# Low parts of half of the up projection's weights by an accumulating DMA instead of GpSimd subtractions

## The chip, the cores and the metric

One core of one Trainium2 chip runs the whole kernel in one launch. The metric is the device time of that launch in microseconds (us). The kernel before took 1085.0 us, the median of three runs (1084.67 to 1085.46 us).

## What is computed

The reference is one layer of an encoder trunk over 512 tokens of width 1024, all in float32: token mixing (a Mamba-2 branch and a windowed attention branch, merged by gates), then channel mixing. The change touches the channel mixing alone, a squared-ReLU MLP with an inner width of 4096:

```
h = rmsnorm(x, pre_mlp_norm[l])
f = jnp.square(jax.nn.relu(h @ w_mlp_in[l])) @ w_mlp_out[l]
x = x + rmsnorm(f, post_mlp_norm[l])
```

`h @ w_mlp_in` is called the up projection (weights 1024 x 4096) and the product with `w_mlp_out` (4096 x 1024) the down projection.

## The kernel before

**Split products.** TensorE multiplies in the type `fp32r`, whose values hold fewer bits than float32. So each float32 operand is split in two: a high part `hi`, the value rounded to `fp32r`, and a low part `lo = value - hi`. A product of two split operands is three matmuls (`mm3`, L404; the matmul itself is issued at L398): high times high, high times low, low times high. For weights, ScalarE (ACT) makes the high part by a cast, and GpSimd (POOL) the low part by a subtraction.

**Up projection.** `up_quantum` (L1491) computes one block of 128 of the 4096 inner columns for all 512 tokens. Its weights are one chunk: 1024 x 128 values, held as a tile of 128 partitions x 1024 (eight blocks of 128 rows side by side), 512 KB. SyncE (SP) loads the chunk into a raw tile `wr` (`chunk_raw`, L445). `chunk_split` (L455) casts it into `wh` (L473) and subtracts into `wl` in four pieces of 128 x 256 (L477). Then `cm` (L527) runs 24 matmuls of 128 x 512 into one PSUM bank `pp`: for each of eight blocks two with `wh` and one with `wl`. So the first matmul that needs `wl` is the third of the 24. `up_done` (L1441) applies the squared ReLU and `combine` (L1457) prepares and splits the operands of the down projection.

**Down projection.** It runs in four parts of 1024 inner columns. Each part is seven products of a fast 2 x 2 block multiplication (`fold`, L1522; a product is 24 matmuls into PSUM banks `ps`), with weight chunks made of raw tiles `wd`, or of `wt`, differences of those; their casts stand at L1571 and their subtractions at L1575.

**Stages.** The up blocks 0 to 7 are computed first. Then the seven products of down part 0 alternate with the up blocks 8 to 15, those of part 1 with blocks 16 to 23, those of part 2 with blocks 24 to 31, and part 3 runs alone at the end. Blocks 16 to 23 lie at about 863 to 956 us of the profile, blocks 24 to 31 at about 956 to 1038 us.

**Buffers.** `wr`, `wh` and `wl` are rings of three buffers each (`RAW` and `SPL` are 3). A chunk can be cast only when TensorE has used the chunk that stood in the same buffer of the ring for the last time, three chunks earlier. Some down chunks are held in other buffers (`twin`) and are made long before they are used.

**Order.** After all instructions are recorded, `Planner` (L77) orders them on every engine by its own model of costs: `depend` (L156) finds what each instruction waits for and in which order the buffers of a ring are taken, `duration` (L205) gives a cost, and `plan` (L264) plays the program through. TensorE's matmuls are taken in program order among those that the model has ready. The order is then fixed, and each engine runs its own list in order.

In the tables below names of buffers carry numbers: `wl_905` is the low part of one chunk, `wh_904` its high part, `pp_911` the bank into which it is multiplied.

Of the kernel before, what the change touches and what calls it, by code (L numbers as in the profile page):

```python
# [10 lines left out]
F32 = mybir.dt.float32  # L11
F32R = mybir.dt.float32r
AF = mybir.ActivationFunctionType
ALU = mybir.AluOpType
# [12 lines left out]
SLOTS, RAW, SPL, PP, AHEAD, SPARE = 67, 3, 3, 3, 4, 6  # L27

LO_MIX = "vp"
LO_DOWN = "p", "p", "p", "vp"  # L30
WARM = 13
LO_V = "pvpvpvpv"
# [44 lines left out]
class Planner:  # L77
# [77 lines left out]

    def depend(self):  # L156
        self.pre = [set() for _ in self.ins]
        live, users, ring, seen, first, base = {}, {}, {}, {}, {}, {}
        self.turn = [set() for _ in self.ins]
        for n, i in enumerate(self.ins):  # L160
            for write, aps in ((False, i.ins), (True, i.outs)):
                for ap in self.operands(aps):
                    name = ap.tensor.name
                    if name.startswith(("in_", "out_")):
                        continue
                    if name not in users:
                        users[name], live[name] = set(), []
                        if name in self.tags:
                            tag, bufs = self.tags[name]
                            held = ring.setdefault(tag, [])  # L170
                            held.append(name)
                            if len(held) > 1:
                                self.turn[n].add(first[held[-2]])
                            first[name] = n
                            if len(held) > bufs:
                                base[name] = users[held[-1 - bufs]]
                                live.pop(held[-1 - bufs])
                    key = (name, ap.offset, tuple(map(tuple, ap.ap)))
                    if key not in seen:
                        seen[key] = self.region(ap)  # L180
                    p0, p1, m = seen[key]
                    kept = []
                    psum = name.startswith(("ps_", "pp_"))
                    for u, w, q0, q1, k in live[name]:
                        hit = q0 < p1 and p0 < q1 and k & m
                        if u != n and (hit and (w or write) or psum):
                            self.pre[n].add(u)
                        if not (u != n and (psum or write and hit and p0 <= q0 and q1 <= p1 and k & ~m == 0)):
                            kept.append((u, w, q0, q1, k))
                    if name in base and not any(u in self.pre[n] for u, *_ in live[name]):  # L190
                        self.pre[n] |= base[name]
                    kept.append((n, write, p0, p1, m))
                    live[name] = kept
                    users[name].add(n)
        self.post, self.next = [[] for _ in self.ins], [[] for _ in self.ins]
        for n, p in enumerate(self.pre):
            p.discard(n)
            self.turn[n] -= p
            self.turn[n].discard(n)
            for u in p:  # L200
                self.post[u].append(n)
            for u in self.turn[n]:
                self.next[u].append(n)

    def duration(self, n):  # L205

        i, e = self.ins[n], self.eng[n]
        outs, ins = self.operands(i.outs), self.operands(i.ins)
        size = lambda ap: math.prod(d[1] for d in list(ap.ap)[1:])
        w = max([size(a) for a in outs + ins])  # L210
        psum = any(a.tensor.name.startswith(("ps_", "pp_")) for a in outs + ins)
        kind = type(i).__name__
        if e == "PE":
            w = size(outs[0])
            if ins[0].dtype == F32R:
                return 13.5 + w / 2.4, False
            c = (2.2 + w / 1.2) if i.is_transpose else (4.4 + w / 0.6)
            return (c / 2 if i.tile_size[1] == 64 and outs[0].ap[0][1] == 64 else c), False
        if e == "SP":
            return (600 if list(outs[0].ap)[0][1] == 64 else 375), False  # L220
        wide = sum(1 for a in ins if size(a) == w and w > 1)
        columns = sum(1 for a in ins if size(a) == 1 and w > 1)
        if e == "ACT" and "DMA" in kind:
            return 400, False
        if e == "ACT":
            c = (170 if psum else 205) + 0.82 * w + (175 if len(outs) > 1 else 0)
            return c + (85 if columns else 0) * (w < 512 or columns > 1), False
        if e == "POOL":
            if "pow" in str(getattr(i, "op", "")):
                return (1020 if w > 1 else 545), True  # L230
            return (190 if w <= 4 else 180 + 2.15 * w), bool(ins)
        if wide >= 2:
            return 158 + 1.04 * w + (45 if columns else 0), not psum
        if kind == "InstTensorScalarPtr" and not psum:
            return 220 + 0.51 * w, True
        return 150 + 1.04 * w, False
# [27 lines left out]
    def plan(self, wait=0.3):  # L264
# [8 lines left out]
        free = dict.fromkeys(self.OVERLAP, 0.0)  # L273
        port = {"DVE": 0.0, "POOL": 0.0}
        queue, kind, landed = 0.0, None, []
        order, self.when = {e: [] for e in self.OVERLAP}, {}
        for _ in self.ins:
            best = None
            for e, some in avail.items():
                if some:  # L280
                    t = max(free[e], min(ready[n] for n in some))
                    if best is None or t < best[0]:
                        best = t, e
            t, e = best
            some = avail[e]
            if e == "PE":
                n = self.next_matmul(some, ready, t, kind)
            else:
                n = min((n for n in some if ready[n] <= t), key=lambda n: (key[n], n))
                m = min(some, key=lambda n: (key[n], n))  # L290
                if ready[m] <= t + wait * self.cost[n][0]:
                    n = m
            some.remove(n)
            order[e].append(n)
            t = self.when[n] = max(t, ready[n])
            c, locks = self.cost[n]
            c *= 2 if e == "PE" and t < self.COLD else 1
            end = t + c
            if e == "SP":
                queue = max(queue, t + self.LEAD) + self.transfer(n)  # L300
                free[e], end = end, queue + self.TAIL
                landed.append(end)
                if len(landed) >= 8:
                    free[e] = max(free[e], sorted(landed)[-8])
            elif e == "PE":
                end += self.change(kind, self.kind[n])
                kind = self.kind[n]
                free[e], end = end, end + 160
            else:
                if locks:  # L310
                    other = "POOL" if e == "DVE" else "DVE"
                    end += max(0.0, port[other] - t - 145)
                    port[e] = end
                free[e] = end - self.OVERLAP[e]
                end += 2500 if "DMA" in type(self.ins[n]).__name__ else 0
            for s in self.post[n]:
                same = self.eng[s] == e == "PE"
                ready[s] = max(ready[s], free[e] if same else end + self.AFTER[self.eng[s]])
                left[s] -= 1
                if not left[s]:  # L320
                    avail[self.eng[s]].append(s)
            for s in self.next[n]:
                ready[s] = max(ready[s], t)
                left[s] -= 1
                if not left[s]:
                    avail[self.eng[s]].append(s)
# [12 lines left out]
class Trunk:  # L339
# [115 lines left out]
    def chunk_split(self, i):  # L455
        if len(self.chunks[i]) == 2:
            self.parts[i] = self.chunks[i][1](i in self.ring)
            return
        _, kk, n, eng = self.chunks[i]
        raw = self.raw.pop(i)  # L460
        m = kk * n
        hi = self.wp.tile([128, 1024], F32R, tag="wh", name=self.name("wh"), bufs=SPL)
# [8 lines left out]
        lo = self.wp.tile([128, 1024], F32R, tag="wl", name=self.name("wl"), bufs=SPL)  # L471
        self.tags[lo.tensor.name] = "wl", SPL
        self.nc.scalar.copy(hi[:, :m], raw)  # L473
        engines = {"v": self.nc.vector, "p": self.nc.gpsimd}
        for e, c in zip(eng, range(0, m, m // len(eng))):
            c = slice(c, c + m // len(eng))
            engines[e].tensor_tensor(lo[:, c], raw[:, c], hi[:, c].bitcast(F32), op=ALU.subtract)  # L477
        v = lambda t: t[:, :m].rearrange("p (k n) -> p k n", k=kk)
# [1010 lines left out]
        return 8 * part + n // 2 + 4 * (n % 2)  # L1489

    def up_quantum(self, i):  # L1491
        return self.cm(self.d_w_mlp_in[0], self.block(i) * 128, lambda: self.h2, lambda ps: self.up_done(ps, i))

    def up_halves(self, n):

# [250 lines left out]
```

## Time and profile before

| | |
|---|---|
| median of three runs | 1085.0 us |
| the profiled execution itself | 1085.44 us |
| its span, first to last instruction | 1083.7 us |
| DVE (VectorE) busy | 785.1 us, 72% |
| ACT (ScalarE) busy | 654.4 us, 60% |
| POOL (GpSimd) busy | 808.1 us, 75% |
| moved by DMA | 152.21 MB, mean 140 GB/s |

The profile is of one execution. Busy time is what an engine spent on instructions. A PE (TensorE) matmul is shown with 0.39 us, from its start to its modelled end, and matmuls overlap; the time that one adds is the distance from one start to the next. PEld is TensorE's weight load, which runs beside the matmuls. A row of the timeline gives start, length, engine, line, operation, tiles (output, arrow, inputs), shape and count, and in brackets the idle time of the engine before it and what ended that. SPq is the queue that issues DMAs.

### The profile page before, as it was taken

Reading aid. Unit: us, or ns where it says so; the run is one execution under the profiler, and the core shown is the slowest. Engines: PE = TensorE matmul, PEld = TensorE weight load, DVE = VectorE, ACT = ScalarE, POOL = GpSimd, SP = SyncE. Lnnn points to the kernel's source line nnn. Section 1 sums busy time; section 2 is a strip of 40 time slices with the busy share of each in tenths; the row PEclk is TensorE's granted clock in tenths of the full one; section 3 lists DMA queues with packets and bytes.
Section 4 is the critical chain, followed back from the end, with each engine's and each line's share of the span. In section 5 each row is a group of like instructions: output and inputs, shape, how many; then the busy total and the mean of one; then the engine's idle time right before and its main releaser. Section 6 shows DMA issues by size and latency. Waiting matters only on the chain.

```text
span 1083.7 us, 16956 instructions
## 1 busy us (share of the span) xinstructions
PE 1073.5 (99%) x5584; PEld 902.2 (83%) x5584; DVE 785.1 (72%) x1345; ACT 654.4 (60%) x1407; POOL 808.1 (75%) x1011
## 2 busy tenths in 40 slices
PE   9999999999999999999999999999999999999997
PEld 8888888888888888888888888889888888888885
DVE  6578787788796787887877558668873755755787
ACT  5566776686865767676686522476755434434443
POOL 4446567557558898989898768566998978978844
PEclk9999999999999999999999999999999999999999
DMA  7444624625536555556564389754722612611522
GB/s 218 118 121 125 150 76 123 146 74 158 131 107 164 149 144 160 158 143 167 136 179 113 103 253 332 226 198 127 237 65 59 201 53 59 198 55 59 161 93 78
DMA packets 221000, 152.21 MB, mean 140 GB/s; under 512 B 12493, under 2 KB 194229, under 8 KB 220912
## 3 DMA queue, kind: packets, MB, share of 16 engines
q1 hardware_dynamic: 220764, 151.06, 48.6%
q8 instruction: 44, 0.72, 0.3%
q14 instruction: 44, 0.36, 0.1%
q10 hardware_dynamic: 148, 0.07, 0.0%
HBM read 138.19 MB, written 12.91 MB: 139 GB/s over the span
## 4 chain that ended last, share of the span: by engine, by line
PE 94%; DVE 2%; DMA 2%; ACT 1%; SPq 1%; issue 1%; POOL 0%; POOLq 0%; DVEq 0%
PE pp L398 66%; PE ps L398 25%; PE ps L402 3%; DMA x<-in_x 1%; DMA wr<-in_w_in 0%; ACT b L423 0%; DVE B L944 0%; DVE x L1401 0%; DVE P L855 0%; DVE x L1655 0%; DVE acc L1621 0%; SPq L383 0%; SPq L570 0%; DVE Q L832 0%; DVE ag L1648 0%
## 5 line engine op out<-in xcount | busy, mean ns | idle before, releaser
L398 PE MATMUL pp<-b,wh 128*128 128x512 f32 (+1 forms) x1840 | 564.8, 388 | 0.2 <-DVE b L424 0.2
L477 POOL TENSOR_TENSOR wl<-wr,wh 128x256 fp32r<-128x256 f32 (+1 forms) x503 | 418.2, 860 | 137.4 <-ACT wh L473 133.9
L398 PEld LDWEIGHTS pp<-b,wh 128*128 128x128 f32 x1840 | 340.2, 188 | 68.2 <-issue 1.5
L398 PE MATMUL pp<-b,wl 128*128 128x512 f32 (+1 forms) x920 | 356.5, 388 | 0.0
L398 PEld LDWEIGHTS pp<-b,wl 128*128 128x128 f32 x920 | 172.9, 188 | 34.3
L473 ACT CAST wh<-wr 128x1024 fp32r<-128x1024 f32 x131 | 136.5, 1042 | 82.0 <-PE pp L398 56.1
L1575 POOL TENSOR_TENSOR wl<-wd,wh 128x256 fp32r<-128x256 f32 x168 | 139.8, 862 | 39.9 <-ACT wh L1571 31.9
L1571 ACT CAST wh<-wd 128x512 fp32r<-128x512 f32 x108 | 63.2, 618 | 53.9 <-PE pp L398 23.8
L398 PE MATMUL ps<-wh,fh 128*128 128x512 f32 (+1 forms) x196 | 75.5, 385 | 0.5 <-DVE acc L1621 0.5
L398 PE MATMUL ps<-wl,fh 128*128 128x512 f32 (+1 forms) x196 | 75.5, 385 | 0.0
L398 PE MATMUL ps<-wh,fl 128*128 128x512 f32 (+1 forms) x196 | 75.4, 385 | 0.0
L1112 ACT ACTIVATE n<-cb,tables 128x128 f32<-128x128 f32 x128 | 48.8, 391 | 26.8 <-DVE cb L1103 22.8
L1449 DVE SCALAR_TENSOR_TENSOR pp<-pp,r 128x512 f32<-128x512 f32 (+1 forms) x31 | 17.5, 565 | 54.0 <-ACT r L1446 53.9
L1575 POOL TENSOR_TENSOR wl<-wt,wh 128x256 fp32r<-128x256 f32 x56 | 45.4, 844 | 9.9 <-ACT wh L1571 6.0
L944 DVE SCALAR_TENSOR_TENSOR u<-pp,cv,u 128x510 f32<-128x510 f32 (+1 forms) x64 | 47.6, 744 | 2.9 <-ACT u L940 1.7
L1042 POOL TENSOR_TENSOR xd<-x,tables 128x256 f32<-128x256 f32 x48 | 35.0, 747 | 19.5 <-ACT x L967 16.9
L1113 ACT ACTIVATE m<-cb,tables 128x128 f32<-128x128 f32 x128 | 48.7, 389 | 0.3 <-DVE cb L1103 0.3
L1148 POOL TENSOR_TENSOR w<-w,E 128x256 f32<-128x256 f32 x48 | 40.3, 852 | 11.1 <-DVE w L1144 5.4
L398 PEld LDWEIGHTS ps<-wh,fh 128*128 128x128 f32 x196 | 36.8, 188 | 8.1 <-DVE acc L1621 0.7
L1108 ACT ACTIVATE rf<-rf,tables 128x128 f32<-128x128 f32 x128 | 41.9, 393 | 2.6 <-DMA rf<-csT 2.6
L398 PEld LDWEIGHTS ps<-wl,fh 128*128 128x128 f32 x196 | 36.8, 188 | 7.4
L398 PEld LDWEIGHTS ps<-wh,fl 128*128 128x128 f32 x196 | 36.8, 188 | 7.2
(301 smaller groups left out, 2085.3 us busy)
## 6 DMA issues: line engine op xcount, KB each, us to landing
wr<-in_w_in SPq DMA_DIRECT2D x74, 512.0 KB, 4.8
wr<-in_w_mlp_in SPq DMA_DIRECT2D x32, 512.0 KB, 4.1
wd<-in_w_mlp_out SPq DMA_DIRECT2D x64, 256.0 KB, 4.7
rb<-csT SPq DMA_DIRECT2D x32, 256.0 KB, 3.9
rf<-csT SPq DMA_DIRECT2D x32, 256.0 KB, 5.5
wr<-in_w_ssd_out SPq DMA_DIRECT2D x14, 512.0 KB, 5.4
wd<-in_w_o SPq DMA_DIRECT2D x28, 256.0 KB, 4.6
E<-csE SPq DMA_DIRECT2D x96, 64.0 KB, 3.9
```

What stands on the lines that cost most here:

```text
L398: self.nc.tensor.matmul(out, lhsT, rhs, start=start, stop=stop, skip_group_check=more)
L402: self.nc.tensor.transpose(out, src, self.ident[:n, :n])
L473: self.nc.scalar.copy(hi[:, :m], raw)
L477: engines[e].tensor_tensor(lo[:, c], raw[:, c], hi[:, c].bitcast(F32), op=ALU.subtract)
L944: nc.vector.scalar_tensor_tensor(u[:, a:e], ps[:, a + d:e + d], self.wtap(t, b), u[:, a:e], op0=ALU.mult, op1=ALU.add)
L1042: nc.gpsimd.tensor_tensor(v4(xd[:, d * 256:(d + 1) * 256]), v4(xs(c)), by_dir(self.coef, c)[:, d].unsqueeze(2).to_broadcast([128, 4, 64]), ...
L1108: nc.scalar.activation(v4(rf)[:, h], v4(rf)[:, h], AF.Identity, bias=ncs[:, 0, h:h + 1])
L1112: nc.scalar.activation(v4(n)[:, h], cb[:, 0], AF.Copy, scale=dt[:, 0, h:h + 1])
L1113: nc.scalar.activation(v4(m)[:, h], cb[:, 1], AF.Copy, scale=dt[:, 1, h:h + 1])
L1148: nc.gpsimd.tensor_tensor(wc, wc, E[:, d], op=ALU.add)
L1571: nc.scalar.copy(hi, w)
L1575: (nc.vector if e == "v" else nc.gpsimd).tensor_tensor(low[:, q], w[:, q], hi[:, q].bitcast(F32), op=ALU.subtract)
```

## The change

For the up blocks 16 to 31 the low part is no longer subtracted on POOL. ScalarE writes the negated high part into `wl` (a copy with scale -1.0, 128 x 1024), and then one DMA, issued from POOL's queue, adds the weights to it, so that `wl` holds value - hi. For blocks 16 to 23 ("dram") the DMA reads the weights from DRAM a second time; for blocks 24 to 31 ("sbuf") it reads the raw tile `wr`. Blocks 0 to 15 keep the subtractions. The planner is told of such a DMA: 1200 ns on POOL, and a landing after a transfer of twice its usual time. Two lines of `depend` now order the buffers of a ring by the instruction that writes them.

```diff
+UP_LO = "pppp", "pppp", "dram", "sbuf"
...
                             if len(held) > 1:
-                                self.turn[n].add(first[held[-2]])
+                                behind[name] = first[held[-2]]
                             first[name] = n
...
+                    if write and name in behind:
+                        self.turn[n].add(behind[name])
...
         if e == "POOL":
+            if "DMA" in kind:
+                return 1200, False
...
+            elif e == "POOL" and "DMA" in type(self.ins[n]).__name__:
+                queue = max(queue, end + self.LEAD) + 2 * self.transfer(n)
+                free[e], end = end, queue + self.TAIL
...
-        _, kk, n, eng = self.chunks[i]
+        src, kk, n, eng = self.chunks[i]
...
         self.nc.scalar.copy(hi[:, :m], raw)
+        if eng in ("dram", "sbuf"):
+            self.nc.scalar.activation(lo[:, :m], hi[:, :m].bitcast(F32), AF.Copy, scale=-1.0)
+            if eng == "dram":
+                self.nc.gpsimd.dma_start(lo[:, :m].rearrange("p (k n) -> p k n", k=kk), src, accum_op=ALU.add)
+            else:
+                self.nc.gpsimd.dma_start(lo[:, :m], raw, accum_op=ALU.add)
+            eng = ""
         engines = {"v": self.nc.vector, "p": self.nc.gpsimd}
-        for e, c in zip(eng, range(0, m, m // len(eng))):
+        for e, c in zip(eng, range(0, m, m // max(len(eng), 1))):
...
     def up_quantum(self, i):
-        return self.cm(self.d_w_mlp_in[0], self.block(i) * 128, lambda: self.h2, lambda ps: self.up_done(ps, i))
+        return self.cm(self.d_w_mlp_in[0], self.block(i) * 128, lambda: self.h2, lambda ps: self.up_done(ps, i), UP_LO[i // 8])
```

What this does to the order of instructions is shown at three places, around the up blocks of `wl_894`, `wl_905` and `wl_910` (the first three of the changed chunks). In the changed kernel the lines of the same statements are higher: a matmul is L406 instead of L398, a cast of an up chunk L481 instead of L473, a cast of a down chunk L1586 instead of L1571, a subtraction of a down chunk L1590 instead of L1575.

TensorE, where the block of `wl_905` begins, before: `pp_911` is this block's bank, and after two matmuls with `wh_904` the first with `wl_905` follows at once.

```order
L398 MATMUL ps_900_9853<-wh_901_9880,fl_1090_9820 128x512
L398 MATMUL pp_911_9989<-b_797_8505,wh_904_9921 128x512
L398 MATMUL pp_911_9989<-b_799_8507,wh_904_9921 128x512
L398 MATMUL pp_911_9989<-b_797_8505,wl_905_9922 128x512
L398 MATMUL pp_911_9989<-b_797_8505,wh_904_9921 128x512
L398 MATMUL pp_911_9989<-b_799_8507,wh_904_9921 128x512
```

TensorE at the same place in the changed kernel; `ps_899` and `ps_900` are banks of a down product.

```order
L406 MATMUL pp_911_9983<-b_797_8505,wh_904_9919 128x512
L406 MATMUL pp_911_9983<-b_799_8507,wh_904_9919 128x512
L406 MATMUL ps_899_9850<-wh_1095_9924,fh_1022_9263 128x512
L406 MATMUL ps_899_9850<-wl_1096_9925,fh_1022_9263 128x512
...
L406 MATMUL ps_900_9851<-wh_1097_9929,fh_1049_9467 128x512
L406 MATMUL ps_900_9851<-wl_1098_9930,fh_1049_9467 128x512
L406 MATMUL pp_911_9983<-b_797_8505,wl_905_9920 128x512
L406 MATMUL pp_911_9983<-b_797_8505,wh_904_9919 128x512
```

Between the second matmul of the block and the first with `wl_905` now stand 17 matmuls of the next down product, which came after the block before. The same was done, with 17 to 19 matmuls, at two more blocks that read from DRAM, and with 15 at three blocks that read the raw tile; one more block of the first kind (with 17) and one of the second (with 10) follow at once upon such a place.

POOL around the same chunks, before: four subtractions for each up chunk (`wl_9922` is the low part of `wl_905`, `wl_9967` that of the down chunk behind it, `wl_9975` that of `wl_910`).

```order
L477 TENSOR_TENSOR wl_9922<-wr_9850,wh_9921 128x256 x4
L1575 TENSOR_TENSOR wl_9967<-wd_9783,wh_9966 128x256 x2
L1575 TENSOR_TENSOR wl_9967<-wd_9785,wh_9966 128x256 x2
L477 TENSOR_TENSOR wl_9975<-wr_9938,wh_9974 128x256 x4
L1575 TENSOR_TENSOR wl_10041<-wt_10042,wh_10040 128x256 x2
```

POOL in the changed kernel; the same tiles are called `wl_9920`, `wl_9963` and `wl_9971`.

```order
L485 DMA wl_9920<-in_w_mlp_in 128x8x128
L1590 TENSOR_TENSOR wl_9963<-wd_9781,wh_9962 128x256 x2
L1590 TENSOR_TENSOR wl_9963<-wd_9783,wh_9962 128x256 x2
L485 DMA wl_9971<-in_w_mlp_in 128x8x128
L1590 TENSOR_TENSOR wl_10035<-wt_10036,wh_10034 128x256 x2
```

One DMA stands where four subtractions stood; what follows it on POOL is the same as before.

ACT around the chunk of `wl_905`, before (`r` is the ReLU of the block that has just ended, `fh` a high part of an operand of the down projection).

```order
L473 CAST wh_9921<-wr_9850 128x1024
L1446 ACTIVATE r_9917<-pp_9892 128x512
L415 CAST fh_10019<-pp_9892 128x256
L1571 CAST wh_9966<-wd_9783 128x512
L1571 CAST wh_9966<-wd_9785 128x512
L473 CAST wh_9974<-wr_9938 128x1024
```

ACT in the changed kernel.

```order
L481 CAST wh_9919<-wr_9848 128x1024
L483 ACTIVATE wl_9920<-wh_9919 128x1024
L1461 ACTIVATE r_9915<-pp_9890 128x512
L423 CAST fh_10013<-pp_9890 128x256
L1586 CAST wh_9962<-wd_9781 128x512
L1586 CAST wh_9962<-wd_9783 128x512
L481 CAST wh_9970<-wr_9934 128x1024
L483 ACTIVATE wl_9971<-wh_9970 128x1024
```

The negated copy stands directly behind the cast whose result it reads, and ahead of the ReLU.

More of the change, by code (lines that the diff above doesn't have):

```diff
@@ L157, in depend @@
         self.pre = [set() for _ in self.ins]
-        live, users, ring, seen, first, base = {}, {}, {}, {}, {}, {}
+        live, users, ring, seen, first, base, behind = {}, {}, {}, {}, {}, {}, {}
         self.turn = [set() for _ in self.ins]
```

## The prediction

> **What bounds the kernel now.** I read the page first, for the busy shares.
>
> ```profile
> span 1083.7 us, 16956 instructions
> PE 1073.5 (99%) x5584; PEld 902.2 (83%) x5584; DVE 785.1 (72%) x1345; ACT 654.4 (60%) x1407; POOL 808.1 (75%) x1011
> PEclk9999999999999999999999999999999999999999
> ```
>
> TensorE (PE) is busy for 1073.5 of 1083.7 us, at full granted clock in every slice. An engine that is busy 99% of the time can only be made to wait, or given less to do, and the change leaves every matmul as it is. Next, who TensorE waits for where the change lies: the changed up blocks run from about 863 to 1038 us, so I asked for its waits from 840 us to the end, and for the busy time by windows.
>
> ```profile
> engine line waited for: us in total, times, longest us
> PE ps L398 <- DVE acc L1621: 0.5, 1, 0.5
> core 0: us, PE busy (x) PEld busy (x) DVE busy (x) ACT busy (x) POOL busy (x), PEclk, DMA share, GB/s
> 863.00:944.00 81.00, 81.00 (x359) 67.11 (x358) 48.86 (x78) 37.12 (x64) 70.05 (x88) 1.00 0.35 103
> 944.00:1026.00 82.00, 82.00 (x364) 67.92 (x363) 50.99 (x81) 37.50 (x66) 69.77 (x88) 1.00 0.30 92
> ```
>
> In the two stages that change, TensorE is busy for all of their 81 and 82 us; the only wait listed, 0.5 us, comes after them. POOL is busy for 70 us of each, much but not all, and never what TensorE waits for. So there is nothing here for a relieved POOL to give back. The whole question is whether the new way of making the low part stays in time, and for that I need the pace of TensorE and the slack of a chunk.
>
> ```profile
> 863.11 10.88 PE pp L398 x48
> ```
>
> This row is of the chain that ended last (start, length, engine, count): 48 matmuls in 10.88 us, 0.2267 us each.
>
> **Slack of the chunks.** From the timeline, the chunk of `wl_905` (cast, subtractions, first matmul with the low part), and the one after it in the same stage, `wl_910`:
>
> ```profile
> 884.81 1.05 ACT L473 CAST wh<-wr 128x1024 fp32r<-128x1024 f32 x1 [4.44 <-PE pp L398]
> 885.94 2.84 POOL L477 TENSOR_TENSOR wl<-wr,wh 128x256 fp32r<-128x256 f32 x4 [3.32 <-ACT wh L473]
> 890.60 0.39 PE L398 MATMUL pp<-b,wl 128*128 128x512 f32 x1
> 890.39 1.05 ACT L473 CAST wh<-wr 128x1024 fp32r<-128x1024 f32 x1 [0.21 <-issue]
> 901.48 0.39 PE L398 MATMUL pp<-b,wl 128*128 128x512 f32 x1
> ```
>
> The cast of the first waited 4.44 us for TensorE to give its buffer back; it ends at 885.86, POOL starts 0.08 us later, and TensorE wants the low part at 890.60, 4.7 us after the cast. I call such a chunk short. The second has 10.0 us, since TensorE runs a down product in between: long. Each of the two stages has three short and five long chunks (long ones start with 894, 910, 924, 940 and 944 in the first stage).
>
> **What goes.** 16 chunks lose four subtractions each, 64 in all, on POOL. TensorE does not wait for POOL in these stages, so this gives 0.
>
> **What comes on ACT.** One copy of 128 x 1024 for each of 16 chunks. The nearest row is the cast of the same size, 1.05 us above: 16.8 us of ACT in all. ACT is busy 37 of 81 us, so it has room. In ACT's list the copy stands directly behind the cast, so it delays the low part by 1.05 us and another 0.08 us for the handover to POOL, and it delays the ReLU behind it. The ReLU's results are operands of the next down part, and the bank that it reads is one of three; the list of TensorE's waits above names neither. That costs 0; with this cover gone it would be 1 us a block.
>
> **What comes as a DMA.** It can be issued at 885.86 + 1.05 + 0.08 = 886.99 us for `wl_905`. TensorE's order has changed with it: the first matmul with `wl_905` has 17 matmuls of the next down product ahead of it that stood behind it before, so it is wanted at 890.60 + 17 x 0.2267 = 894.45. That leaves the DMA **7.46 us** from POOL's start to its landing. For the short chunks that read the raw tile the same sum, with 15 matmuls:
>
> ```profile
> 966.41 1.05 ACT L473 CAST wh<-wr 128x1024 fp32r<-128x1024 f32 x1 [4.44 <-PE pp L398]
> 972.20 0.39 PE L398 MATMUL pp<-b,wl 128*128 128x512 f32 x1
> ```
>
> 966.41 + 1.05 + 1.05 + 0.08 = 968.59, wanted at 972.20 + 15 x 0.2267 = 975.60: **7.01 us**. The long chunk `wl_910` has 901.48 - (890.39 + 2.18) = 8.91 us, with its place unchanged; `wl_894`, one of the tighter long ones, by its rows
>
> ```profile
> 869.08 1.04 ACT L473 CAST wh<-wr 128x1024 fp32r<-128x1024 f32 x1
> 879.72 0.39 PE L398 MATMUL pp<-b,wl 128*128 128x512 f32 x1
> ```
>
> has 879.72 - (869.08 + 2.17) = 8.47 us.
>
> What such a DMA takes is shown by no row: the page has no DMA that POOL issues and none that accumulates. The nearest is the plain load of the same 512 KB, issued by SyncE, in the same stages (queue: packets, MB, share of 16 engines; issues: KB each, median us to landing):
>
> ```profile
> q1 hardware_dynamic: 21115, 18.04, 34.1%
> wr<-in_w_mlp_in SPq DMA_DIRECT2D x14, 512.0 KB, 4.3
> L477 POOL TENSOR_TENSOR wl<-wr,wh 128x256 fp32r<-128x256 f32 x68 | 54.2, 828 | 11.9 <-ACT wh L473 11.7
> ```
>
> Lower end: it takes what a load takes, 4.3 us. Upper end: two loads in turn, 8.6 us, as it has to read the weights and the old contents of `wl`. My value lies between: of the 4.3 us only the transfer doubles. These rows are of 860 to 1035 us, so 18.04 MB kept 16 engines busy for 0.341 x 175 = 59.7 us, and 0.524 MB take 1.73 us. With 0.83 us (one POOL instruction of L477) for POOL to issue it, the DMA takes 4.3 + 1.7 + 0.83 = **6.8 us**, the same for both sources; the tile as a source has longer runs and might be quicker.
>
> So the short chunks have 7.46 - 6.8 = 0.6 us and 7.01 - 6.8 = 0.2 us to spare, the long ones 1.6 us and more: TensorE does not wait. This is a narrow pass, and the upper end fails it.
>
> [...]
>
> **What moves.** Up to 22 matmuls of the next down product now come before the rest of an up block. The first need of that product's last chunk, `wl_908`, moves from 31 matmuls after the block's start to 9, to about 892.2 us by the rows above. Its two first subtractions (2 x 0.74 us) stand behind the DMA in POOL's list, so POOL must have issued the DMA by 890.6, 3.6 us after 886.99. At 0.83 us it has; if issuing took longer than that, the DMA itself would be late by more, so this adds no wait of its own. SyncE's load into a raw tile that the DMA reads can start some 5 us later than after the subtractions; it is hidden by its lead:
>
> ```profile
> 888.80 0.38 SPq L453 DMA_DIRECT2D wr<-in_w_mlp_in  x1
> 907.63 2.83 POOL L477 TENSOR_TENSOR wl<-wr,wh 128x256 fp32r<-128x256 f32 x4 [2.08 <-ACT wh L473]
> ```
>
> The load issued at 888.80 follows at once on the subtractions of `wl_905`, and its chunk is subtracted at 907.63, 18.8 us later, against 4.3 us to land. DMA engines are used 34% here; 16 more transfers of 512 KB, at twice 1.73 us, add 16 x 3.46 / 175 = 32%.
>
> **Sum.** 0 removed from TensorE's path, 0 added: the profiled execution took 1083.7 us of span and 1085.4 us in all, the median of the runs is 1085.0. I forecast 1085.3 us.
>
> **Rivals.**
> *The low part lands late (slower).* If the DMA takes longer than 7.46 us (from DRAM) or 7.01 us (from the tile), TensorE stands at the third matmul of each short block, and nothing catches up, since a stalled TensorE also gives its buffers back later. Each us over costs 3 us in each stage, and past about 8.5 to 8.9 us the ten long chunks add theirs. At the upper end, 8.6 us: 3 x 1.14 + 3 x 1.59 + 0.1 = 8.3 us, 1093.7 us. At 9.2 us: 5.2 + 6.6 + some 5 = 17 us, 1102 us. It passes my bound at about 7.6 us. For it: a spare of 0.2 to 0.6 us against 4.3 us of unknown. Against it: the lower end. Chance 0.35.
>
> *POOL's issue is held up by VectorE (slower).* The subtractions show that the two engines can block each other:
>
> ```profile
> L477 POOL TENSOR_TENSOR wl<-wr,wh x68: 726/740/1197, 859.6 to 1024.7; 128x256 fp32r<-128x256 f32 x68
> 891.21 1.21 DVE L1536 TENSOR_TENSOR wt<-wd,wd 128x512 f32<-128x512 f32 x1 [0.18 <-POOL wl L1575]
> ```
>
> The same piece takes 0.73 to 1.20 us (least, median, most in ns), and so does VectorE's work. If an issue waits out one such VectorE instruction, the DMA takes 6.8 + 1.2 = 8.0 us: 3 x 0.57 + 3 x 1.02 = 4.8 us, 1090 us. Against it: not each of the six short chunks meets one. Chance 0.12. [...]
>
> *TensorE gains.* The most that a wait could give back from 840 us on is the 0.5 us above, 1085 us. Only a pace below 0.2267 us would show. Chance 0.03.
>
> **Chances and range.** No wait: 0.50, with a range of its own from 1084.4 to 1087.0. A measurement can tell about 0.2% (2.2 us) from no change. Faster 0.03, within 0.2% 0.50, slower 0.35 + 0.12 = 0.47. The range reaches from 1084.3, just under the lowest run, to 1102, a DMA of 9.2 us; I leave about 0.15 beyond it.
>
> **What would show it.** TensorE's waits from 840 us on should stay near 0.5 us, with no row that names a DMA into `wl`; POOL's busy time should fall by 64 x 0.83 = 53 us, less what 16 issues take; ACT's should rise by 16.8 us. The median time to landing of the DMAs into `wl`, from the page's part on issues, is the number that decides: under 7 us I am right, over 7.6 us the first rival is. A wait of TensorE at `pp` on a DMA, in three places of a stage, is that rival's mark; POOL instructions of unequal length at L485 and L487 are the second's. A slower pace of TensorE without waits would make all of this wrong.

## The result and the profile after

The changed kernel took **1096.8 us** (median of four runs, 1095.24 to 1097.78) against 1085.23 us for the kernel before on the same chip (four runs, 1084.67 to 1085.55): a ratio of 1.0106, 95% interval 1.0088 to 1.0123. It is slower by 11.6 us. That lies inside the range of the prediction, but the likeliest case, no wait, did not come. The profiled execution is the quickest of the four, 1095.24 us, with a span of 1093.4 us, so its trace holds 9.7 us of the loss.

First the page of the changed kernel, the busy times and the two queues (packets, MB, share of 16 engines):

```profile
PE 1077.7 (99%) x5584; PEld 902.4 (83%) x5584; DVE 778.1 (71%) x1345; ACT 671.5 (61%) x1423; POOL 777.4 (71%) x963
q1 hardware_dynamic: 220764, 151.06, 48.4%
q0 software_dynamic: 9472, 8.39, 5.3%
```

POOL lost 30.7 us of work and ACT gained 17.1 us. The queue of POOL's DMAs is new: 16 times 0.524 MB. TensorE is still "99%" busy; the loss can't be seen in that number, since 9.7 us are 0.9% of the span. It is seen in TensorE's waits, here from 855 us to the end:

```profile
PE pp L406 <- DMA wl<-in_w_mlp_in: 3.2, 1, 3.2
PE ps L406 <- ACT wh L1586: 1.4, 1, 1.4
PE pp L406 <- DMA wl<-wr: 0.5, 1, 0.5
PE ps L406 <- DVE acc L1636: 0.5, 1, 0.5
```

Before there was only the last row. Three new waits have come, each of them once: one at a DMA from DRAM, one at a DMA from the tile, and one at a cast of a down chunk. The DMAs themselves, by line (least, median and most, in ns and then in us to landing):

```profile
L485 POOL DMA_DIRECT2D wl<-in_w_mlp_in x8: 1554/1563/1805, 870.9 to 951.2; - x8
...
DMA to landing us min/median/max: 6.6/7.0/11.1
...
L487 POOL DMA_DIRECT2D wl<-wr x8: 856/871/924, 959.9 to 1034.2; - x8
...
DMA to landing us min/median/max: 4.5/5.6/8.3
```

The medians are 7.0 and 5.6 us, close to the 6.8 us forecast. The largest is not: 11.1 us. It belongs to block 21 (`wl_935`, the third short chunk of its stage), whose DMA was issued at 930.9 us. TensorE there:

```profile
938.50 0.39 PE L406 MATMUL ps<-wh,fh 128*128 128x512 f32 x1
942.09 0.80 PE L406 MATMUL pp<-b,wl 128*128 128x512 f32 x1 [3.21 <-DMA wl<-in_w_mlp_in]
942.68 1.06 PE L406 MATMUL pp<-b,wh 128*128 128x512 f32 x2
...
945.97 0.62 PE L406 MATMUL pp<-b,wh 128*128 128x512 f32 x2
...
949.85 0.61 PE L406 MATMUL pp<-b,wh 128*128 128x512 f32 x2
951.87 0.73 PE L406 MATMUL ps<-wh,fh 128*128 128x512 f32 x2 [1.41 <-ACT wh L1586]
```

The low part was wanted at 938.73 (938.50 + 0.2267), 7.8 us after its issue, and came 3.4 us late. Two more losses hang on this. First, the matmuls behind the wait are slow: two of them show as 1.06 us at 942.68 and as 0.62 us at 945.97. Windows of 1 us show why (the columns as in the prediction; after POOL come the granted clock, the DMA share and GB/s; the share adds up the times of all pieces that the 16 engines moved, and where these overlap it passes 1):

```profile
941.00:942.00 1.00, 0.00 (x0) 0.00 (x0) 0.99 (x3) 0.00 (x0) 0.00 (x0) 0.96 1.15 344
942.00:943.00 1.00, 0.91 (x2) 0.81 (x3) 1.00 (x2) 0.00 (x0) 0.00 (x0) 0.50 1.23 281
...
944.00:945.00 1.00, 1.00 (x4) 0.81 (x3) 0.00 (x0) 0.00 (x0) 0.00 (x0) 0.50 1.38 213
945.00:946.00 1.00, 1.00 (x6) 0.79 (x5) 0.00 (x0) 0.00 (x0) 0.00 (x0) 0.84 1.22 158
```

At the end of the wait TensorE's granted clock fell to 0.50, and it stayed there for some 3.4 us. Second, at 951.87 TensorE waits 1.4 us for the cast of a down chunk, the first need of the next product, which the new order pulls ahead of block 22's low part. ACT at that time:

```profile
948.68 1.05 ACT L481 CAST wh<-wr 128x1024 fp32r<-128x1024 f32 x1 [9.59 <-PE pp L406]
949.77 1.06 ACT L483 ACTIVATE wl<-wh 128x1024 fp32r<-128x1024 f32 x1
950.74 0.58 ACT L1461 ACTIVATE r<-pp 128x512 f32<-128x512 f32 x1
951.21 1.13 ACT L1586 CAST wh<-wd 128x512 fp32r<-128x512 f32 x2
```

The cast at 951.21 stands behind block 23's cast, the new negated copy and a ReLU, and the first of these had to wait for the stalled TensorE to free its buffer.

Added up from the distances between matmuls beyond 0.2267 us each: 3.4 us of wait at block 21, 1.8 us of slow matmuls behind it, 1.6 us at the cast, 0.7 us at block 31 (the DMA that landed after 8.3 us), 0.3 us at `acc` and about 1.4 us in small steps of 0.1 to 0.2 us. That is 9.1 us; before, these steps were all absent (the old wait of 0.5 us at `acc`, which is in both, is not counted). Three quarters of it come from one DMA.

Why that DMA? SyncE's queue around it, in the changed kernel, shows the loads of the next down part's weights:

```profile
922.78 5.64 SPq L1576 DMA_DIRECT2D wd<-in_w_mlp_out  x6
929.36 0.38 SPq L461 DMA_DIRECT2D wr<-in_w_mlp_in  x1
931.85 1.80 SPq L1576 DMA_DIRECT2D wd<-in_w_mlp_out  x4
...
937.78 0.80 SPq L1576 DMA_DIRECT2D wd<-in_w_mlp_out  x2
```

And the trace of before, in windows, for the same place:

```profile
863.00:920.00 57.00, 57.00 (x253) 47.23 (x252) 32.23 (x51) 26.12 (x46) 47.30 (x60) 1.00 0.22 67
...
925.00:930.00 5.00, 5.00 (x23) 4.14 (x23) 2.37 (x3) 3.03 (x5) 5.00 (x7) 1.00 0.91 306
...
935.00:940.00 5.00, 5.00 (x23) 4.13 (x22) 2.24 (x3) 0.69 (x3) 5.00 (x7) 1.00 0.73 208
```

The 0.35 that the prediction read for the whole stage is a mean of 0.22 over 57 us and of a burst with up to 0.91. Blocks 21 and 22 have their DMAs in the burst.

### The profile page after: what moved, and what is told of

Same layout as the page of the kernel before. It is cut to its first block, busy times and chain, and to the rows that moved or that the text cites. A ratio compares the mean times of both kernels' runs of the same rounds, so it can differ in the third digit from the quotient of the medians.

```text
span 1093.4 us, 16937 instructions
## 1 busy us (share of the span) xinstructions
PE 1077.7 (99%) x5584; PEld 902.4 (83%) x5584; DVE 778.1 (71%) x1345; ACT 671.5 (61%) x1423; POOL 777.4 (71%) x963
## 4 chain that ended last, share of the span: by engine, by line
PE 91%; DMA 3%; DVE 2%; issue 1%; ACT 1%; POOL 1%; SPq 0%; DVEq 0%; POOLq 0%; ACTq 0%
PE pp L406 65%; PE ps L406 23%; PE ps L410 3%; DMA wr<-in_w_in 1%; DMA wl<-in_w_mlp_in 1%; DMA wl<-wr 1%; DMA x<-in_x 0%; ACT wh L481 0%; ACT b L431 0%; DVE x L1670 0%; DVE B L959 0%; DVE acc L1636 0%; POOL wl L1590 0%; DVE x L1416 0%; DMA hot<-in_hot 0%
## 5 line engine op out<-in xcount | busy, mean ns | idle before, releaser
L406 PE MATMUL pp<-b,wh 128*128 128x512 f32 (+1 forms) x1840 | 565.6, 389 | 0.2 <-DVE b L432 0.2
L492 POOL TENSOR_TENSOR wl<-wr,wh 128x256 fp32r<-128x256 f32 (+1 forms) x439 | 368.8, 869 | 124.7 <-ACT wh L481 118.2
L406 PEld LDWEIGHTS pp<-b,wh 128*128 128x128 f32 x1840 | 340.8, 188 | 68.5 <-issue 1.5
L406 PE MATMUL pp<-b,wl 128*128 128x512 f32 (+1 forms) x920 | 357.3, 389 | 3.7 <-DMA wl<-in_w_mlp_in 3.2
L406 PEld LDWEIGHTS pp<-b,wl 128*128 128x128 f32 x920 | 173.2, 188 | 39.2 <-DMA wl<-in_w_mlp_in 3.6
L481 ACT CAST wh<-wr 128x1024 fp32r<-128x1024 f32 x131 | 136.5, 1042 | 88.0 <-PE pp L406 56.9
L1590 POOL TENSOR_TENSOR wl<-wd,wh 128x256 fp32r<-128x256 f32 x168 | 140.0, 899 | 46.9 <-ACT wh L1586 41.5
L1586 ACT CAST wh<-wd 128x512 fp32r<-128x512 f32 x108 | 63.2, 618 | 57.2 <-PE pp L406 28.8
L406 PE MATMUL ps<-wh,fh 128*128 128x512 f32 (+1 forms) x196 | 75.0, 387 | 2.1 <-ACT wh L1586 1.4
L406 PE MATMUL ps<-wl,fh 128*128 128x512 f32 (+1 forms) x196 | 75.7, 387 | 0.0
L406 PE MATMUL ps<-wh,fl 128*128 128x512 f32 (+1 forms) x196 | 75.3, 385 | 0.0
L1590 POOL TENSOR_TENSOR wl<-wt,wh 128x256 fp32r<-128x256 f32 x56 | 46.5, 895 | 22.3 <-ACT wh L1586 19.8
L1636 DVE TENSOR_TENSOR acc<-acc,ps 128x512 f32<-128x512 f32 (+1 forms) x49 | 32.9, 671 | 29.2 <-PE ps L406 28.7
L406 PEld LDWEIGHTS ps<-wh,fh 128*128 128x128 f32 x196 | 36.7, 188 | 10.8 <-ACT wh L1586 1.8
L406 PEld LDWEIGHTS ps<-wl,fh 128*128 128x128 f32 x196 | 36.8, 188 | 8.7 <-POOL wl L1590 1.5
```

The lines of the kernel that those rows point to most:

```text
L406: self.nc.tensor.matmul(out, lhsT, rhs, start=start, stop=stop, skip_group_check=more)
L1586: nc.scalar.copy(hi, w)
L1590: (nc.vector if e == "v" else nc.gpsimd).tensor_tensor(low[:, q], w[:, q], hi[:, q].bitcast(F32), op=ALU.subtract)
L1636: self.nc.vector.tensor_tensor(self.acc[t, j][:, c], self.acc[t, j][:, c], ps[:, c], op=ALU.add)
```

## Experiments

In all of them the list `UP_LO` has one entry for each of the 32 up blocks instead of one for eight:

```diff
-        return self.cm(self.d_w_mlp_in[0], self.block(i) * 128, lambda: self.h2, lambda ps: self.up_done(ps, i), UP_LO[i // 8])
+        return self.cm(self.d_w_mlp_in[0], self.block(i) * 128, lambda: self.h2, lambda ps: self.up_done(ps, i), UP_LO[i])
```

The main theory (A in the expectations) is that a few DMAs in the burst make the loss, above all block 21's, with what follows from it. The texts name the theories that each run sets against it.

**Block 21 back on POOL.**

```diff
+UP_LO = ["pppp"] * 16 + ["dram"] * 5 + ["pppp"] + ["dram"] * 2 + ["sbuf"] * 8
```

> Block 21 (the chunk of wl_935) gets its four subtractions back, the other 15 DMAs stay. Theory A (one DMA fell into the burst of down loads, landed after 11.1 us, and that wait with its after-effects is nearly all of the loss): TensorE's 3.2 us wait goes, the time falls to 1086 to 1090 us; what may be left is a wait of up to 2 us at block 22, whose DMA falls into the same burst. Theory B (a loss spread over all changed blocks, by ACT's copies, the new order or POOL): one part in 16 goes, the time stays above 1094 us.

Measured: 1090.43 us (1090.25 to 1090.97) against 1085.22 us for the kernel before (13 runs); ratio 1.0046, 1.0031 to 1.0061. TensorE's waits:

```profile
PE pp L406 <- DMA wl<-in_w_mlp_in: 1.9, 2, 1.4
PE pp L406 <- DMA wl<-wr: 0.9, 1, 0.9
```

Taking one chunk of 16 back removes 6.4 of the 11.6 us, about the 6.7 us that the trace puts down to block 21 and its followers. The time is just above the range expected: the burst now makes blocks 22 and 23 late. Block 23's DMA landed after 11.4 us, and TensorE, no longer delayed, waits there.

**Only block 21.**

```diff
+UP_LO = ["pppp"] * 21 + ["dram"] + ["pppp"] * 10
```

> Block 21 alone has a DMA from DRAM, the other 15 have their subtractions. Theory A: the DMA lands 10 to 12 us after its issue, TensorE waits some 3 us and runs some 3 us at a lowered clock behind it; 1090 to 1096 us. Theory B (spread over the blocks): 1085 to 1087 us.

Measured: 1091.70 us (1090.6 to 1092.24), ratio 1.0055, 1.004 to 1.007. One single accumulating DMA costs 6.5 us. TensorE's waits have one new row:

```profile
PE pp L406 <- DMA wl<-in_w_mlp_in: 5.4, 1, 5.4
```

And the DMA, among the issues (KB, us to landing):

```profile
wl<-in_w_mlp_in POOLq DMA_DIRECT2D x1, 512.0 KB, 12.6
```

There is no other DMA of POOL's beside it, so the 12.6 us aren't made by the 16 DMAs among themselves, and the 1085 to 1087 us of B are out. The time lies in the range expected, but the landing and the wait are longer than the 10 to 12 us and some 3 us that I had expected.

**All 16 from the raw tile.**

```diff
+UP_LO = ["pppp"] * 16 + ["sbuf"] * 16
```

> All 16 DMAs read the raw tile, in 128 pieces of 4096 bytes instead of 1024 of 512. Theory A with taking of turns by pieces: in the burst such a DMA gives way 8 times on each DMA engine instead of 64 times and lands in 6 to 8.5 us; waits of 0 to 2 us, 1086 to 1090 us. Theory C (the bytes in the burst alone count): block 21 lands after 10 us and more as before, and the time stays above 1092 us.

Measured: 1088.09 us (ten runs, 1087.42 to 1089.1), ratio 1.0023, 1.0014 to 1.0033. The one new wait of TensorE:

```profile
PE pp L406 <- DMA wl<-wr: 0.6, 1, 0.6
```

The DMAs, by their line:

```profile
L487 POOL DMA_DIRECT2D wl<-wr x16: 859/874/1095, 870.9 to 1026.8; - x16
...
DMA to landing us min/median/max: 4.5/5.7/8.5
```

With the tile as the source, no block in the burst makes TensorE wait; block 21's DMA landed after 5.6 us. What is left is block 31, at 8.5 us. The other source takes away 8.7 us of the 11.6.

But it also changes what runs beside block 21's DMA, which is issued at 930.73 here. SyncE's queue:

```profile
931.86 2.95 SPq L1576 DMA_DIRECT2D wd<-in_w_mlp_out  x4
936.40 0.38 SPq L461 DMA_DIRECT2D wr<-in_w_mlp_in  x1
```

The load at 936.40 overwrites the raw tile that the DMA reads, so it waits until the DMA has landed; in the changed kernel the same load is issued at 929.36. And of the four loads issued from 931.86 on, no piece moves before 935.5. So 0.3 MB of loads moved between this DMA's issue and its landing, against 2.2 MB in the changed kernel. The run shows what the other source is worth, but not that longer pieces are the reason, and it does not decide between A and C, since the bytes beside the DMA are not the same. Why the four loads stood still is not shown.

**The same without block 31.**

```diff
+UP_LO = ["pppp"] * 16 + ["sbuf"] * 15 + ["pppp"]
```

> Blocks 16 to 30 by DMAs from the raw tile, block 31, the only one that TensorE waited for with all 16 from the tile, by subtractions. Theory A: no DMA is waited for, 1085 to 1087 us, within 0.2% of the kernel before. Theory B (a part of the loss is spread): 1087.5 us or more.

Measured: 1086.01 us (eleven runs, 1085.55 to 1088.52) against 1085.45 us (16 runs); ratio 1.0003, 0.9994 to 1.0012. From 855 us on TensorE has its old wait only:

```profile
PE ps L406 <- DVE acc L1636: 0.5, 1, 0.5
```

The page's busy times:

```profile
PE 1074.2 (99%) x5584; PEld 901.6 (83%) x5584; DVE 776.7 (72%) x1345; ACT 671.1 (62%) x1422; POOL 772.1 (71%) x966
```

So here 15 of the 16 chunks are made by DMAs without a wait, POOL has 36 us less work than before, and nothing is gained: no version of it that was run beats the kernel before.

**The planner isn't told of the DMA.** The DMAs are those of the change, but the planner counts nothing for them, so TensorE's order stays that of before, without matmuls of the next product ahead of the low part.

```diff
             if "DMA" in kind:
-                return 1200, False
+                return 0, False
...
-                queue = max(queue, end + self.LEAD) + 2 * self.transfer(n)
-                free[e], end = end, queue + self.TAIL
+                free[e] = end
```

> The planner is told that the DMA costs nothing, so TensorE's order is that of the kernel before; the DMAs are the same 16. Theory A (a wait is the time to landing less the slack): the six short blocks have 3.6 us from issue to need, so waits of about 3.4 us at two blocks from DRAM, 7 us at block 21, 1 to 2 us at three blocks from the tile, with lowered clock behind the long ones: 1102 to 1112 us. Theory D (pulling matmuls of the next product ahead is itself what costs): 1085 to 1092 us.

Measured: 1110.90 us (1110.29 to 1112.22), ratio 1.0237, 1.022 to 1.0254. TensorE's waits on DMAs (lines are one lower in this kernel):

```profile
PE pp L405 <- DMA wl<-in_w_mlp_in: 13.5, 3, 6.9
PE pp L405 <- DMA wl<-wr: 4.1, 3, 2.1
```

Now each of the six short chunks waits, three in each stage, at the places that the prediction named for its first rival. Moving matmuls ahead is worth 14 us; it isn't what made the change slow.

**A plain copy instead of the accumulating one.** The low part then holds the whole weight.

```diff
-                self.nc.gpsimd.dma_start(lo[:, :m].rearrange("p (k n) -> p k n", k=kk), src, accum_op=ALU.add)
+                self.nc.gpsimd.dma_start(lo[:, :m].rearrange("p (k n) -> p k n", k=kk), src)
...
-                self.nc.gpsimd.dma_start(lo[:, :m], raw, accum_op=ALU.add)
+                self.nc.gpsimd.dma_start(lo[:, :m], raw)
```

> The 16 DMAs copy instead of accumulating, so that the low part holds the whole weight (the subtraction is left out). Theory A (accumulating costs a second read of each piece, and the rest is as for a load): a 512-byte piece takes 27 ns as in a load instead of 66, the median time to landing falls from 7.0 to 4.5 to 5.2 us from DRAM and from 5.6 to 3.5 to 5 us from the tile; block 21 waits for at most 1.5 us; 1086 to 1090 us. Theory E (the time is POOL's 1.6 us of issuing and a fixed latency of such a DMA): from DRAM it still lands after 6.3 us or more.

Measured: 1089.68 us (three runs, 1089.21 to 1092.76), ratio 1.0041, 1.0024 to 1.0058. The DMAs of both lines:

```profile
L485 POOL DMA_DIRECT2D wl<-in_w_mlp_in x8: 919/920/1135, 870.8 to 949.7; - x8
...
DMA to landing us min/median/max: 5.0/5.6/10.0
...
L487 POOL DMA_DIRECT2D wl<-wr x8: 528/570/597, 958.5 to 1032.4; - x8
...
DMA to landing us min/median/max: 2.9/3.1/7.2
```

Accumulating costs 1.4 us (from DRAM) and 2.5 us (from the tile) of the median, part of it in issuing (1563 against 920 ns, 871 against 570). But block 21's DMA still takes 10.0 us, and TensorE still waits, 2.3 us there and 1.4 us at the cast behind it. I had expected at most 1.5 us and was wrong, and both medians lie outside the ranges expected. (The trace is of the slowest of the three executions, 1092.76 us.) The burst costs a plain copy (10.0 against a median of 5.6 us) as much as an accumulating one (11.1 against 7.0).

**The burst by itself.** Block 17 is a quieter place: in the changed kernel 0.8 MB of loads moved between its DMA's issue and its landing. Here it alone is made by a DMA from DRAM, and ten loads of 256 KB, which nothing reads, are added on SyncE's queue beside it.

```diff
+UP_LO = ["pppp"] * 17 + ["dram+"] + ["pppp"] * 14
...
+        if eng[-1] == "+":
+            eng = eng[:-1]
+            self.held_back(self.burst)
...
+    def burst(self):
+        for k in range(10):
+            b = self.dp.tile([128, 512], F32, name=f"burst{k}")
+            self.nc.sync.dma_start(b, self.d_w_mlp_out[0, k * 128:(k + 1) * 128, :512])
```

> Block 17 (wl_905, landing after 7.0 us in the changed kernel) alone has a DMA from DRAM, and ten loads of 256 KB in runs of 2 KB, whose results nobody reads, are put beside it. Theory A (turns with the packets of other loads): it lands 10 to 13 us after its issue, as block 21 does. Theory F (block 21 is late for another reason of its place, such as VectorE holding POOL up): it lands after 7.5 us or less. The planner moves it 32 matmuls back, so the time itself says little.

Measured: 1086.2 us (one run). The issues by form, with KB and median us to landing:

```profile
burst<-in_w_mlp_out SPq DMA_DIRECT2D x10, 256.0 KB, 5.6
wl<-in_w_mlp_in POOLq DMA_DIRECT2D x1, 512.0 KB, 11.4
```

In the changed kernel the DMA of this block lands after 7.0 us. With 2.1 MB of loads beside it, it takes 11.4 us, as long as block 21's, and TensorE waits 0.8 us for it. Added loads alone are enough to make a DMA that late, at another place than block 21's; the 7.5 us or less of theory F did not come. This is the run that shows the cause, in one execution.

**The same with the raw tile as the source** (`"sbuf+"` in place of `"dram+"`).

> The same ten loads beside block 17, whose DMA now reads the raw tile. Theory A with turns by pieces (8 of 4096 bytes on each DMA engine instead of 64 of 512): it lands 5.5 to 7.5 us after its issue. Theory C (the bytes beside it alone count): 9 us or more.

Measured: 4.7 us to landing, 1085.71 us (one run). This says nothing on how a burst acts on such a DMA: SyncE's queue held the added loads back behind a load into a raw tile that had to wait for this very DMA, and by the records no load ran beside it. With all 16 from the tile the same was seen at block 21.

So the pair was tried once more, at block 18, with 16 loads started from block 17, which stays on POOL.

```diff
+UP_LO = ["pppp"] * 17 + ["pppp+", "sbuf"] + ["pppp"] * 13
```

> Block 18 (wl_910) alone has a DMA, from the raw tile; sixteen loads of 256 KB in runs of 2 KB, which nobody reads, are issued from about 889 us on, so that its DMA at about 893 us stands among them. Without them it lands after 6.2 to 6.4 us there. Turns by pieces (8 of 4096 bytes on each DMA engine): 6.5 to 8.5 us. The bytes beside it alone: as long as the next kernel's, 10 us or more.

> The same with block 18's DMA from DRAM, which lands after 6.6 to 6.9 us without the loads. Turns by pieces (64 of 512 bytes): 10 to 13 us, at least 3 us more than from the tile. The bytes alone: both within 1.5 us of each other.

The second is the same with `"dram"` for `"sbuf"`. Measured, first the tile, then DRAM:

```profile
wl<-wr POOLq DMA_DIRECT2D x1, 512.0 KB, 7.6
```

```profile
wl<-in_w_mlp_in POOLq DMA_DIRECT2D x1, 512.0 KB, 9.9
```

Without added loads this block's DMA lands after 6.4 us (from the tile, in the run with all 16 from the tile) and 6.8 us (from DRAM, in the changed kernel), with 0.5 MB of loads beside it in both. The added loads cost 1.2 and 3.1 us, with some 1.3 and 1.7 MB beside the DMA. From DRAM it was 2.3 us slower than from the tile, at 9.9 us; I had expected 10 us or more and 3 us or more, and a theory that counts bytes alone a difference of 1.5 us or less. The result lies between. Times were 1085.06 and 1085.64 us against 1085.44 us, one run each.

The records of the single pieces tell what differs. The DMA from DRAM consists of 1024 pieces of 512 bytes (64 for each of 16 engines, if they are spread evenly), the one from the tile of 128 pieces of 4 KB (8 for each). In the changed kernel a piece of block 21's DMA takes no longer in the burst than one of block 16's, which has no load beside it (a median of 65 ns in both), but fewer of them move: from 934 to 939 us 133 to 210 in each us, with 26 to 111 pieces of 2 KB of loads, against 243 to 351 from 874 to 877 us. The turns of the expectations were a supposition of mine, that the DMA gives way to loads at each of its pieces, 64 times from DRAM and 8 times from the tile; no run shows it. The 3.1 against 1.2 us agree in direction with it, but the two had unequal traffic beside them, so that the number of pieces is the reason is argued and not shown.

## Why the prediction was half right

**What held.** TensorE bounds these stages, and a relieved POOL gives nothing back: with the waits gone (1086.01 against 1085.45 us) the 36 us that POOL saves are worth 0 within the interval. ACT's copies took 1062 ns in the median, and ACT has 17.1 us more, against 16.8 us forecast. The 6.8 us for a quiet DMA lies between the medians measured, 7.0 and 5.6 us. That it is so close is partly luck, since its terms were off: the issue takes 1.56 us from DRAM, not the 0.83 us taken from a subtraction, and the transfer, put at 3.5 us, is an estimated 4.2 us from DRAM (64 pieces of 66 ns on an engine) and 2.7 us from the tile (8 of 341 ns). The windows of the short chunks, 7.46 and 7.01 us, were right: in the changed kernel block 17 had 7.4 us from the issue to the first matmul with its low part, and its DMA, landing after 7.0 us, was not waited for.

**The step that failed** is "the same for both sources", one time D for all 16 DMAs, with a spare of 0.2 to 0.6 us measured against that one time. Its terms were means and medians over 175 us: a load's 4.3 us, and a transfer worked out from "34.1%" of the DMA engines. In the burst the share of the kernel before is already 0.91 for 5 us. In the changed kernel it is above 1 there, and block 21's DMA takes 11.1 us, where its chunk had 7.8 us. The time of a transfer has to be read from the window in which it will run, as was done for TensorE. The sign that the prediction called decisive, a median time to landing under 7 us, could not show this either: the medians are 7.0 and 5.6 us, and the loss comes from the longest one. Of the raw tile the prediction said that the next load into it starts later and that this is hidden; it did, and with all 16 from the tile this also kept loads away from block 21's DMA.

**The first rival** had the mechanism, a low part that lands late, and its mark, a wait at `pp` on a DMA. But it priced it as a shift of all DMAs ("each us over costs 3 us in each stage"), where one DMA was 3.4 us late and one 0.7 us; block 22's, 10.8 us to landing, was in time only because TensorE was late by then, and the others were in time anyway. That its 1093.7 to 1102 us hold the result is thus partly chance. "Nothing catches up" held: the span grew by 9.7 us for 9.1 us of listed steps.

**Two prices that the prediction lacked.** The clock: 1.8 us for slow matmuls behind a wait of 3.4 us. And "this adds no wait of its own", said of the down chunks whose first need moves ahead: it was worked out for `wl_908` only, in a quiet place. After the stall the same move makes TensorE wait 1.4 us for a cast, in the changed kernel and with the plain copy alike.

**The second rival**, POOL's issue held up by VectorE, left no mark where it was looked for. That subtractions on POOL and VectorE's work can slow each other, the trace of before shows: VectorE's L1536 takes 0.68 to 0.69 us where no subtraction runs beside it (at 906.02, 987.62 and 1031.95 us) and up to 1.31 us beside them, and of the 68 subtractions of L477 the 14 that took 1.00 to 1.20 us all ran beside VectorE's L1536 or L1537, while the 20 with nothing of VectorE's beside them took 0.73 to 0.75 us. But the issues from the tile take 856 to 924 ns, those from DRAM 1554 to 1805 ns, and only the first of them took the 1805 ns. At block 31, though, the first piece of the DMA moves 3.65 us after the issue, against 1.4 to 1.6 us for the other seven from the tile. The windows there:

```profile
1035.00:1036.00 1.00, 1.00 (x7) 0.81 (x6) 1.00 (x3) 1.00 (x3) 0.65 (x2) 1.00 1.06 260
1036.00:1037.00 1.00, 1.00 (x6) 0.84 (x5) 1.00 (x3) 0.52 (x2) 1.00 (x2) 1.00 0.63 104
1037.00:1038.00 1.00, 1.00 (x6) 0.84 (x5) 0.96 (x4) 0.00 (x0) 1.00 (x2) 1.00 0.84 250
```

The issue was at 1034.25, so the DMA might have started at about 1035.8. VectorE is busy throughout, but loads run there too, so whether these or VectorE delay the start stays open; it was not tried. Loads can do it: beside the added loads block 17's DMA from DRAM moved its first piece 4.4 us after the issue instead of 2.3 us, with VectorE about as busy in both, and block 18's from the tile after 2.9 us instead of 1.6 us. In the run with all 16 from the tile, the DMAs of blocks 22 and 23 also started late, by up to 2 us.

## What to carry to other kernels

A DMA that stands between two engines on the critical path must be priced at the busiest window in which it can run, not at the mean share of its stage; look for prefetch bursts, such as the loads of a next part's weights, and read the DMA share in windows of a few us. If it has to be there, try a source on the chip: here the DMAs from the raw tile landed sooner than the second reads of DRAM (medians of 5.6 and 7.0 us in the changed kernel), and a tile that such a DMA holds also holds back the loads that would overwrite it (one was issued at 936.40 us, with all 16 from the tile, instead of 929.36 us). And relieving an engine that was 75% busy, but that TensorE did not wait for, was worth nothing here, though 36 us of work went.

## What the runs showed of the hardware

**The clock after a wait.** In the changed kernel TensorE's clock was at 0.50 for 3.4 us after the wait of 3.2 us. After the waits of 5.4 us (only block 21) and 6.9 us (the planner untold) it was at 0.50 for 6.8 us, a part of it while TensorE still stood. The slow matmuls cost some 1.5 to 2 us each time, in addition to the wait. With the plain copy, after a wait of 2.3 us, TensorE's rows show it again; the clock is 0.99 in the window from 940 to 941 us and 0.50 in the next two:

```profile
940.58 0.50 PE L406 MATMUL pp<-b,wl 128*128 128x512 f32 x1 [2.31 <-DMA wl<-in_w_mlp_in]
940.92 0.99 PE L406 MATMUL pp<-b,wh 128*128 128x512 f32 x2
941.71 0.63 PE L406 MATMUL pp<-b,wl 128*128 128x512 f32 x1
```

Waits of 1.4 us and one of 2.1 us (with the planner untold) left the matmuls at full pace. So from 855 us on the shortest wait that the lowered clock followed was 2.3 us, and the longest that it did not follow 2.1 us; what decides it between the two, no run shows.

**Pieces.** By the records of single pieces, 512 bytes take about 27 ns in a plain load on SyncE's queue, 44 to 47 ns in a quiet plain copy on POOL's and 66 ns in an accumulating one (means); 4 KB from the tile take 176 and 341 ns. Issuing an accumulating DMA took POOL 0.87 us from the tile (128 pieces) and 1.56 us from DRAM (1024 pieces); whether the pieces or the source make the difference was not separated.
